# A two-layer attention trunk on one core: another order of blocks in paired weight groups, one weight sum on VectorE, side work behind the splits

## The chip, the core and the metric

One core of a Trainium2 chip runs the whole program. The metric is device time in microseconds (us); three runs were made, and one more execution was recorded by the hardware profiler. TensorE is the matrix engine, VectorE (DVE) and ScalarE (ACT) the elementwise engines, GpSimd is POOL, SyncE is SP; SBUF is the on-chip memory, PSUM holds TensorE's sums in eight banks.

## What is computed

A decoder trunk of two layers on 256 tokens of width 2048 in float32: one of gated linear attention (GLA, 4 heads), one of retention (8 heads). Cut to what matters here:

```python
def gla_mixer(h, w_in, w_a1, w_a2, b_a, head_g, w_out):
    q, k, v, gate = jnp.split(h @ w_in, [GLA_DK, 2 * GLA_DK, 2 * GLA_DK + D_INNER], axis=-1)
    ...                                   # decayed attention in chunks, norm of each head
    return (o * jax.nn.silu(gate)) @ w_out

def retention_mixer(h, positions, w_in, gn_g, gn_b, w_out):
    q, k, v, gate = jnp.split(h @ w_in, [RET_DK, 2 * RET_DK, 2 * RET_DK + D_INNER], axis=-1)
    q, k = apply_rotary(q, cos, sin), apply_rotary(k, cos, sin)
    ...                                   # scores with per-head decay, group norm of each head
    return (o * jax.nn.silu(gate)) @ w_out

for i in range(2):
    h = h + (gla_mixer, retention_mixer)[i](rms_norm(h, g[i]), ...)
return rms_norm(h, final_norm)
```

Nearly all of the work is the four large products with weights (`h @ w_in`, `o @ w_out` in each layer).

## The kernel before

**Weights.** All weights lie in HBM as groups of 2048 x 512. A group is four chunks of 512 rows (1 MB, tile `raw`, four buffers, loaded by SP's queue at L183). A chunk is two units of 256 rows, tiles 128x1024. A unit is split into two reduced-precision parts: `hi` by a copy on ScalarE (L216), `lo = raw - hi` on VectorE (L217); three buffers each. A product of exact factors is then three products (hi with hi, lo with hi, hi with lo: L277 to L279 in pairs). Units are numbered in the order in which they are used (`hi287`, `lo287`). `next_weights` writes the splits up to two units ahead of the products. A scheduler with a model of the engines sets the final order on each engine; each engine then works its queue in order.

**Groups and pairs.** Some groups are multiplied plainly (`group_w` for queries and keys, `rqk` in retention; `group_x`). Others come as pairs of groups gp and gq: for the upper half of the 2048 rows, the 2x2 block product of two token halves and two groups is made with seven products instead of eight. A list of blocks says the order: V0 to V3 and G0 to G3 are ordinary blocks of gp and gq over the lower half of the rows (each one unit, both token halves, 12 matmuls of 512 columns), S1 to S7 the seven products (each one chunk, so two units, one combination of tokens, also 12 matmuls). So an ordinary block needs one split, a seven-product block two.

The seven products need sums of weight chunks. They are made in place: after a chunk's unit is split, POOL issues a transfer of 0.5 MB from HBM that adds into the `raw` buffer (`accum_op`, L225). Buffer x holds gp's chunk 0 for S1, then with gq's chunk 0 added for S5, then with gq's chunk 1 for S6, then with gp's chunk 1 for S4. Buffer y holds gq's chunk 1 for S3, then with gq's chunk 0 for S7. S2 uses gp's chunk 1. With the two lower chunks of each group (V0/V1, V2/V3, G0/G1, G2/G3) a pair has seven chunks. There are 13 pairs: six in retention heads (value and gate groups, `rp`), seven in the output products (`ga`, `gb`: GLA's first and second half of inner columns; `ra`, `rb`: retention's), two per half but one in `rb`, whose other two groups are multiplied plainly.

**Sums in PSUM.** `pair_x` uses banks c11, c21, c12 (pool `acc`, four) and a, b (pool `lev`, two). S1's result in a is copied to c11 by ScalarE (L375), and V0 and S2 add there. Other partial results go to the caller's `on` function, which in the output half adds them to the residual (L916, L883) and in retention makes values and gates from them.

**Side work.** Rotary and scores (`ret_scores`), the head's norm (`o_part`), the transposes of its output (`og_part`, `transpose_out`) and the sums of tokens for pairs (`token_combos`) are generators in the queue `side`; `advance` runs one step after each unit or block. The scheduler is free to put such a step on ScalarE or VectorE ahead of splits. `o_part` of a paired head runs at once, at the first unit of the next head's `rqk`.

**Residual.** After each pair of the halves `gb` and `ra` half of the residual (1 MB) is stored to HBM (`held`, L931), because the buffer is used for the token sums `x1`, `x2` in between; it comes back at L1137.

Of the kernel before, what the change touches and what calls it, by code (L numbers as in the profile page):

```python
# [17 lines left out]
P = 128  # L18
# [37 lines left out]
def kernel(  # L56
# [63 lines left out]
    PAIR = ("S1", "V0", "S2", "V1", "S5", "S3", "V2", "G0", "S6", "G1", "S7", "V3", "S4", "G2", "G3")  # L120

    def plan_pair(gp, gq):
# [7 lines left out]
        for block in PAIR:  # L130
            kind, n = block[0], int(block[1])
            if kind in "VG":
                j, half = divmod(n, 2)
                c = chunk(kind + str(j), gp if kind == "V" else gq, 2 + j)
                units.append((c, half, half == 1, ()))
            elif n == 2:
                plan_units(plan_chunk(gp, 1))
            elif n in (3, 7):
                plan_units(chunk("y", gq, 1), n == 7, [(gq, 0)] if n == 3 else ())
            else:  # L140
                then = {1: [(gq, 0)], 5: [(gq, 1)], 6: [(gp, 1)], 4: ()}[n]
                plan_units(chunk("x", gp, 0), n == 4, then)

    def plan_all():
        g = 0
        for stage, heads in (("gla", 2), ("gla", 2), ("ret", 4), ("ret", 4)):
            for h in range(heads):
                plan_group(g)
                if stage == "ret" and h < heads - 1:
                    plan_pair(g + 1, g + 2)  # L150
                    g += 3
                    continue
# [4 lines left out]
            plan_pair(g, g + 1)  # L157
# [3 lines left out]
            else:  # L161
                plan_pair(g + 2, g + 3)
# [41 lines left out]
    def emit_split(pieces=1, between=None):  # L204
# [9 lines left out]
        for k in range(pieces):  # L214
            sl = slice(k * step, (k + 1) * step)
            a = nc.scalar.activation(hi[:, sl], src[:, sl], AF.Copy)  # L216
            b = nc.vector.tensor_tensor(lo[:, sl], src[:, sl], hi[:, sl].bitcast(F32), ALU.subtract)  # L217
            if i == 0:
# [11 lines left out]
    state = {"sub": 0}  # L230
    side = deque()

    def advance(n=1):
        for _ in range(n):
            while side:
                try:
                    next(side[0])
# [36 lines left out]

    def product(ps, a, hi, lo, q, start, stop):
        xh, xl = a
        mm(ps, xh, hi[:, q, :], start=start, stop=False, skip_group_check=True)  # L277
        mm(ps, xh, lo[:, q, :], start=False, stop=False, skip_group_check=True)  # L278
        mm(ps, xl, hi[:, q, :], start=False, stop=stop, skip_group_check=True)  # L279
# [46 lines left out]
    def pair_x(lhs, name, cname, on, late=None):  # L326

        a = lev_p.tile([P, GW], F32, tag="lev", name=f"{name}_psa")
        c11 = acc_p.tile([P, GW], F32, tag="acc", name=f"{name}_ps11")

        def seven(ps, get, start, stop):
            for half in range(2):
                hi, lo = next_weights()
                for q in range(SUB):
                    k = half * SUB + q
                    product(ps, get(k), hi, lo, q, start and k == 0, stop and k == CHUNK - 1)
# [5 lines left out]
        def mixed(n):  # L342
            return lambda k: tuple(x[:, k] for x in combos[cname][n])

        def both(ps, j, start, stop, second_first=False):
            hi, lo = next_weights()
            order = [(q, t) for q in range(SUB) for t in range(2)]
            if second_first:
                order = [(q, t) for t in (1, 0) for q in range(SUB)]
            for q, t in order:  # L350
                kt = 2 * CHUNK + j * SUB + q
                x = tuple(lhs[:, kt, i, t * P : (t + 1) * P] for i in range(2))
                product(ps[t], x, hi, lo, q, start[t] and q == 0, stop[t] and q == SUB - 1)
            advance()

        c21 = b = c12 = None
        for block in PAIR:
            kind, n = block[0], int(block[1])
            if kind == "V":
                if c21 is None:  # L360
                    c21 = acc_p.tile([P, GW], F32, tag="acc", name=f"{name}_ps21")
                if n == 2 and late is not None:
                    late()
                both((c11, c21), n, (False, n == 0), (n == 3, False), n == 0)
                if n == 3:
                    on("11", c11)
            elif kind == "G":
                both((c12, b), n, (False, False), (n == 3, n == 3))
                if n == 3:
                    on("12", c12)  # L370
                    on("22", b)
            elif n == 1:
                seven(a, plain(0, 0), True, True)
                with tc.high_priority():
                    nc.scalar.activation(c11, a, AF.Copy)  # L375
            elif n == 2:
                seven(c11, plain(1, 0), False, False)
            elif n == 5:
                while cname not in combos:
                    advance()  # L380
                b = lev_p.tile([P, GW], F32, tag="lev", name=f"{name}_psb")
                seven(b, mixed(0), True, True)
                on("q", b)
            elif n == 3:
                c12 = acc_p.tile([P, GW], F32, tag="acc", name=f"{name}_ps12")
                seven(c12, mixed(2), True, False)
            elif n == 6:
                seven(a, mixed(1), False, True)
                on("p2", a)
            elif n == 7:  # L390
                seven(a, mixed(3), False, True)
                on("p3", a)
# [37 lines left out]
    def evac_w(ps, dst, name):  # L430
        tmp = t4_p.tile([P, 4, SEQ], F32, tag="t4", name=f"{name}_h2")
        with tc.high_priority():
# [219 lines left out]
    def transpose_out(src, kt0, scale0, dst, name):  # L652
        for half in range(2):
# [7 lines left out]
            for jj in range(2):  # L661
                kt = kt0 + half * 2 + jj
                if scale0 is None:
                    nc.scalar.activation(dst[:, kt, 0, :], tp[:, jj, :], AF.Copy)
                    nc.vector.tensor_tensor(
                        dst[:, kt, 1, :], tp[:, jj, :], dst[:, kt, 0, :].bitcast(F32), ALU.subtract
                    )
                else:
# [222 lines left out]
    def out_half(first, final, name, later=None, keep_resid=False):  # L891
# [13 lines left out]
        for pair in range(1 if final else 2):  # L905
# [5 lines left out]
            def on(event, ps):  # L911
# [126 lines left out]
    def ret_scores(h, box):  # L1038
# [5 lines left out]
        nc.vector.tensor_tensor(a, qk, tb(0, 4), ALU.mult)  # L1044
        nc.vector.tensor_tensor(four(b)[:, :, 0, :], four(qk)[:, :, 1, :], tb(1, 2), ALU.mult)
        yield
        nc.vector.tensor_tensor(four(b)[:, :, 1, :], four(qk)[:, :, 0, :], tb(1, 2), ALU.mult)
        nc.vector.tensor_tensor(four(a)[:, :, 0, :], four(a)[:, :, 0, :], four(b)[:, :, 0, :], ALU.subtract)
# [9 lines left out]
        yield  # L1058
# [16 lines left out]
    def ret_head(h):  # L1075
# [6 lines left out]

        ps = group_w(xhl, f"rqk{h}", hook=late_o)
# [5 lines left out]
        evac_w(ps, qk, f"rqk{h}")  # L1089
# [10 lines left out]
        def o_part(v, o, bank):  # L1100
            drain_side()
            po = o_mms(hw["sc"], v, f"ro{h}", bank)
            if o is None:
                o = o_p.tile([P, 2, GW], F32, tag="o", name=f"ro{h}")
            bs = st_p.tile([P, 2, 6], F32, tag="bs", name=f"bs{h}")
            mv = st_p.tile([P, 2, 2], F32, tag="mv", name=f"mv{h}")
            for t in range(2):
# [4 lines left out]
                )  # L1112
# [190 lines left out]
```

## Time and profile before

| | before |
|---|---|
| runs, us | 1411.2, 1412.0, 1413.4 (median 1412.0) |
| profiled execution, us | 1413.7, span 1412.0 |
| granted TensorE clock, mean | 0.997 |
| TensorE / VectorE / ScalarE busy | 98% / 74% / 57% |
| transfers | 316.04 MB, mean 224 GB/s |

A group row of the profile reads: line, engine, operation, output <- inputs by the program's names, shape, count; then busy us, mean ns of one, idle us before. A row of waits: engine, line of the waiting instruction, what it waited for, us in total, times, longest. A row of transfers: names, queue, count, KB each, median us from issue to landing. A timeline row starts with start and duration in us and ends, in brackets, with the idle time before it and what ended it; a row of the chain of waits has start, duration, engine, name and line. A row of windows: the stretch, its length, busy us (and instructions) of TensorE, its weight loads, VectorE, ScalarE and GpSimd, the granted clock, the DMA engines' share, GB/s.

### The profile page before, as it was taken

The numbers are of one execution on the slowest core, as the hardware profiler recorded it, in microseconds if no ns is written. First come the engines' busy times: TensorE is split into PE (matmuls) and PEld (weight loads), VectorE is DVE, ScalarE is ACT, GpSimd is POOL, SyncE is SP. The second block draws the span as 40 slices with busy tenths as digits, with TensorE's granted clock in tenths as the row PEclk, the third lists the DMA queues.
The fourth block names the chain that finished last, engine by engine and source line by source line (L and its number), as shares of the span: only waits on it lengthen the run. The fifth ranks groups of instructions, "written<-read, shape, count | busy, mean of one in ns | idle before, by whom it ended". The sixth has DMA issues, their size and how long they took to land.

```text
span 1412.0 us, 17904 instructions
## 1 busy us (share of the span) xinstructions
PE 1380.2 (98%) x6644; PEld 1149.6 (81%) x6644; DVE 1037.8 (74%) x1477; ACT 800.6 (57%) x1019; POOL 190.6 (13%) x361
## 2 busy tenths in 40 slices
PE   8999999999999999999999999999899999999997
PEld 7888888778888888877888888887787878788877
DVE  6594887777845785788878787887667777778773
ACT  6665655654555656666655555455456565654563
POOL 1011030110000020211102020111101212110200
PEclk9999999999999999999999999999999999999999
DMA  9554555998555555799687969569988787874981
GB/s 349 207 183 145 197 173 179 205 285 271 175 171 184 184 186 180 197 301 283 207 269 204 264 201 325 199 195 271 240 297 219 254 219 256 228 305 164 225 295 62
DMA packets 54631, 316.04 MB, mean 224 GB/s; under 512 B 6400, under 2 KB 6912, under 8 KB 25232
## 3 DMA queue, kind: packets, MB, share of 16 engines
q1 hardware_dynamic: 34944, 243.42, 47.7%
q0 software_dynamic: 18592, 70.13, 24.3%
q10 hardware_dynamic: 1008, 1.35, 0.3%
q8 instruction: 52, 0.85, 0.2%
q14 instruction: 35, 0.29, 0.1%
HBM read 308.58 MB, written 6.29 MB: 223 GB/s over the span
## 4 chain that ended last, share of the span: by engine, by line
PE 74%; DMA 11%; DVE 7%; issue 4%; ACT 3%; POOL 1%; ACTq 0%; POOLq 0%; DVEq 0%
DMA raw<-in_w_all 11%; PE rqk_ps L421 8%; PE gv_ps L256 4%; PE gv_ps L257 4%; PE gv_ps L258 4%; DVE lo L217 4%; PE gg_ps L256 4%; PE rqk_ps L422 4%; PE gg_ps L258 4%; PE gg_ps L257 4%; PE gqk_ps L421 3%; ACT hi L216 2%; PE rp__ps L278 2%; PE rp__ps L279 2%; PE rp__ps L277 2%
## 5 line engine op out<-in xcount | busy, mean ns | idle before, releaser
L217 DVE TENSOR_TENSOR lo<-raw,hi 128x1024 fp32r<-128x1024 f32 (+1 forms) x551 | 667.0, 1223 | 294.0 <-ACT hi L216 288.8
L216 ACT ACTIVATE hi<-raw 128x1024 fp32r<-128x1024 f32 (+1 forms) x551 | 578.5, 1057 | 490.4 <-PE rqk_ps L421 86.5
L421 PE MATMUL rqk_ps<-xhl,hi 128*128 128x512 f32 x480 | 162.0, 396 | 0.0
L225 POOL DMA_DIRECT2D raw<-in_w_all x104 | 88.6, 852 | 390.4 <-DVE lo L217 370.9
L422 PE MATMUL rqk_ps<-xhl,lo 128*128 128x256 f32 x480 | 121.9, 282 | 0.0
L421 PEld LDWEIGHTS rqk_ps<-xhl,hi 128*128 128x128 f32 x480 | 87.7, 188 | 16.7
L257 PE MATMUL gv_ps<-lo,xhl 128*128 128x512 f32 x256 | 100.4, 392 | 0.0
L257 PE MATMUL gg_ps<-lo,xhl 128*128 128x512 f32 x256 | 100.4, 392 | 0.0
L258 PE MATMUL gv_ps<-hi,xhl 128*128 128x512 f32 x256 | 100.3, 392 | 0.0
L258 PE MATMUL gg_ps<-hi,xhl 128*128 128x512 f32 x256 | 100.0, 391 | 0.0
L256 PE MATMUL gv_ps<-hi,xhl 128*128 128x512 f32 x256 | 93.0, 391 | 0.0
L422 PEld LDWEIGHTS rqk_ps<-xhl,lo 128*128 128x128 f32 x480 | 87.9, 188 | 5.0
L256 PE MATMUL gg_ps<-hi,xhl 128*128 128x512 f32 x256 | 91.7, 391 | 0.0
L278 PE MATMUL rp__ps<-lo,xhl 128*128 128x512 f32 x192 | 75.8, 395 | 5.8 <-DVE lo L217 5.8
L279 PE MATMUL rp__ps<-hi,xhl 128*128 128x512 f32 x192 | 74.8, 390 | 0.0
L277 PE MATMUL rp__ps<-hi,xhl 128*128 128x512 f32 x192 | 71.7, 394 | 2.9 <-ACT rp__ps L375 2.9
L421 PE MATMUL gqk_ps<-xhl,hi 128*128 128x512 f32 x216 | 72.2, 396 | 0.0
L789 POOL TENSOR_TENSOR s<-s,m 128x64 f32<-128x64 f32 x56 | 32.3, 610 | 241.0 <-DVE m L780 187.9
L257 PEld LDWEIGHTS gv_ps<-lo,xhl 128*128 128x128 f32 x256 | 48.1, 188 | 9.7
L257 PEld LDWEIGHTS gg_ps<-lo,xhl 128*128 128x128 f32 x256 | 48.1, 188 | 9.6
L256 PEld LDWEIGHTS gv_ps<-hi,xhl 128*128 128x128 f32 x256 | 47.9, 188 | 9.9
L258 PEld LDWEIGHTS gg_ps<-hi,xhl 128*128 128x128 f32 x256 | 48.1, 188 | 9.6
(503 smaller groups left out, 2772.2 us busy)
## 6 DMA issues: line engine op xcount, KB each, us to landing
raw<-in_w_all SPq DMA_DIRECT2D x225, 1024.0 KB, 5.1
raw<-in_w_all POOLq DMA_DIRECT2D x104, 512.0 KB, 8.4
held<-resid POOLq DMA_DIRECT2D x4, 1024.0 KB, 8.2
resid<-held POOLq DMA_DIRECT2D x2, 2048.0 KB, 12.1
resid<-in_x_n SPq DMA_DIRECT2D x2, 1024.0 KB, 12.6
gg<-in_gn_g POOLq DMA_DIRECT2D x8, 256.0 KB, 4.1
gb<-in_gn_b POOLq DMA_DIRECT2D x8, 256.0 KB, 3.9
raw<-in_w_all SPq DMA_DIRECT2D x3, 512.0 KB, 6.7
```

The source lines that it names most:

```text
L216: a = nc.scalar.activation(hi[:, sl], src[:, sl], AF.Copy)
L217: b = nc.vector.tensor_tensor(lo[:, sl], src[:, sl], hi[:, sl].bitcast(F32), ALU.subtract)
L225: nc.gpsimd.dma_start(src, chunk_src(g, k)[:, rows], accum_op=ALU.add)
L256: mm(ps, xh, hi[:, q, :], start=kt == 0, stop=False)
L257: mm(ps, xh, lo[:, q, :], start=False, stop=False)
L258: mm(ps, xl, hi[:, q, :], start=False, stop=kt == NKT - 1)
L277: mm(ps, xh, hi[:, q, :], start=start, stop=False, skip_group_check=True)
L278: mm(ps, xh, lo[:, q, :], start=False, stop=False, skip_group_check=True)
L279: mm(ps, xl, hi[:, q, :], start=False, stop=stop, skip_group_check=True)
L421: mm(ps[c], wh, rhs[:, kt, :, :], start=kt == 0, stop=False)
L422: mm(ps[c][:, 0, :], wl, rhs[:, kt, 0, :], start=False, stop=False)
L789: nc.gpsimd.tensor_tensor(dst, dst, side_of(m[:, li, :]), ALU.add)
```

## The change

- Three block orders take the place of one. LATE (the first pair of an output half) and EARLY (the second) and SLOW (the retention heads) alternate ordinary and seven-product blocks.
- In LATE and EARLY the sum for S6 is x + y on VectorE, in two halves of 128x1024, when both S3 and S5 have been split; y then takes its own addition. In SLOW all additions stay with POOL.
- S1's result no longer goes to c11 by a copy: the caller takes it (`p1`), in the output half by an addition to the residual, in retention by an eviction to SBUF that is added when c11 is complete. Where G0 comes before S5 (LATE), the second output bank is one of its own and S5's result is added to the residual twice.
- From the first retention head on, side work and the eviction of `rqk` are held behind the latest split on ScalarE and VectorE; rotary, norm and output work are cut into more steps, and `o_part` goes to the side queue.
- `transpose_out` evicts two tiles at once where there is no scale. The residual is stored once per half, 2 MB.

```diff
-    PAIR = ("S1", "V0", "S2", "V1", "S5", "S3", "V2", "G0", "S6", "G1", "S7", "V3", "S4", "G2", "G3")
+    LATE = ("V0", "S1", "V1", "S2", "G0", "S5", "G1", "S3", "V2", "S6", "V3", "S7", "G2", "S4", "G3")
+    EARLY = ("V0", "S1", "V1", "S3", "V2", "S5", "V3", "S6", "G0", "S2", "G1", "S7", "G2", "S4", "G3")
+    SLOW = ("V0", "S1", "V1", "S3", "V2", "S5", "V3", "S2", "G0", "S6", "G1", "S7", "G2", "S4", "G3")
...
+        x, y = (gp, 0), (gq, 1)
+        both = None if order is SLOW else max(order.index("S3"), order.index("S5"))
...
+            elif pos == both:
+                then = [(at["x"], at["y"]), (at["y"], (gq, 0))]
+            elif both is None and n == 5:
+                then = [(at["x"], y)]
+            elif both is None and n == 3:
+                then = [(at["y"], (gq, 0))]
...
-        for g, k in then:
-            rows = slice(j * SUB, (j + 1) * SUB)
-            nc.gpsimd.dma_start(src, chunk_src(g, k)[:, rows], accum_op=ALU.add)
+            latest[:] = [a.ins, b.ins]
+        rows = slice(j * SUB, (j + 1) * SUB)
+        for to, what in then:
+            x = raws[to][:, rows]
+            if isinstance(what, int):
+                nc.vector.tensor_tensor(x, x, raws[what][:, rows], ALU.add)
+            else:
+                nc.gpsimd.dma_start(x, chunk_src(*what)[:, rows], accum_op=ALU.add)
...
+    def behind_splits():
+        with tc.issue_after(latest[0]), tc.issue_after(latest[1]):
+            yield
...
-                    next(side[0])
+                    with behind_splits() if state["behind"] else nullcontext():
+                        next(side[0])
...
-                with tc.high_priority():
-                    nc.scalar.activation(c11, a, AF.Copy)
+                on("p1", bank["a"])
...
+                shared = "22" not in bank
+                on("q", bank["b"], shared)
...
-            for jj in range(2):
-                kt = kt0 + half * 2 + jj
-                if scale0 is None:
-                    nc.scalar.activation(dst[:, kt, 0, :], tp[:, jj, :], AF.Copy)
...
+            if scale0 is None:
+                d = dst[:, kt0 + half * 2 : kt0 + half * 2 + 2]
+                nc.scalar.activation(d[:, :, 0, :], tp, AF.Copy)
+                nc.vector.tensor_tensor(d[:, :, 1, :], tp, d[:, :, 0, :].bitcast(F32), ALU.subtract)
...
+                if event == "p1":
+                    join(0, 0, ALU.add)
+                elif event == "q":
                     join(0, 1, ALU.subtract)
+                    if not shared:
+                        join(1, 1, ALU.add)
...
-            pair_x(ogt, f"{name}{pair}", name, on, drain_side)
-            if keep_resid:
-                cols = slice(2 * pair * GW, (2 * pair + 2) * GW)
-                nc.gpsimd.dma_start(held[:, :, cols], R["t"][:, :, cols])
+            pair_x(ogt, f"{name}{pair}", name, on, EARLY if pair else LATE, drain_side)
+        if keep_resid:
+            nc.gpsimd.dma_start(held, R["t"])
...
+        state["behind"] = True
         ps = group_w(xhl, f"rqk{h}", hook=late_o)
...
-        evac_w(ps, qk, f"rqk{h}")
+        with behind_splits() if paired else nullcontext():
+            evac_w(ps, qk, f"rqk{h}", not paired)
...
+            if event == "p1":
+                with tc.high_priority():
+                    nc.scalar.activation(o[:, 1, :], ps, AF.Copy)
+            elif event == "q":
...
             elif event == "11":
-                split_scaled(v[:, 0], ps, r2[:, 0:1])
+                with tc.high_priority():
+                    tt(o[:, 1, :], ps, o[:, 1, :], ALU.add)
+                split_scaled(v[:, 0], o[:, 1, :], r2[:, 0:1])
...
-        pair_x(xhl, f"rp{h}_", "x1" if h < 4 else "x2", on)
+        pair_x(xhl, f"rp{h}_", "x1" if h < 4 else "x2", on, SLOW)
...
-            o_part(v, o, (lev_p, "lev"))
+            side.append(o_part(v, o, (lev_p, "lev")))
```

What the change moves is seen in the order on the engines. First VectorE at the start of the second retention head's pair, before: `lo286` and `lo287` are S1's units, `lo288` is V0's; `rqk1` is the eviction of queries and keys, `rot0` the transposes of the head ahead, `ra1` and `rb1` the rotary.

```order
L217 TENSOR_TENSOR lo287_6391<-raw123_6283,hi287_6390 128x1024
L435 TENSOR_TENSOR rqk1_6411<-rqk1_ps0_6176,rqk1_h2_6412 128x256
L665 TENSOR_TENSOR ogt_107<-rot0_tp0_6245,ogt_107 128x256
L665 TENSOR_TENSOR ogt_107<-rot0_tp1_6274,ogt_107 128x256
L435 TENSOR_TENSOR rqk1_6411<-rqk1_ps1_6177,rqk1_h2_6412 128x256
L435 TENSOR_TENSOR rqk1_6411<-rqk1_ps2_6178,rqk1_h2_6412 128x256
L665 TENSOR_TENSOR ogt_107<-rot0_tp0_6245,ogt_107 128x256
L435 TENSOR_TENSOR rqk1_6411<-rqk1_ps3_6179,rqk1_h2_6412 128x256
L665 TENSOR_TENSOR ogt_107<-rot0_tp1_6274,ogt_107 128x256
L1044 TENSOR_TENSOR ra1_6454<-rqk1_6411,trig_108 128x1024
L1045 TENSOR_TENSOR rb1_6455<-rqk1_6411,trig_108 128x2x256
L1047 TENSOR_TENSOR rb1_6455<-rqk1_6411,trig_108 128x2x256
```

There `lo288` follows. After the change, at the same place (`lo287` and `lo288` are S1's units, V0's `lo286` stands ahead):

```order
L233 TENSOR_TENSOR lo287_6392<-raw124_6311,hi287_6391 128x1024
L473 TENSOR_TENSOR rqk1_6412<-rqk1_ps0_6180,rqk1_h2_6413 128x256
L702 TENSOR_TENSOR ogt_107<-rot0_tp0_6333,ogt_107 128x2x256
L702 TENSOR_TENSOR ogt_107<-rot0_tp1_6360,ogt_107 128x2x256
L473 TENSOR_TENSOR rqk1_6412<-rqk1_ps1_6181,rqk1_h2_6413 128x256
L473 TENSOR_TENSOR rqk1_6412<-rqk1_ps2_6182,rqk1_h2_6413 128x256
L473 TENSOR_TENSOR rqk1_6412<-rqk1_ps3_6183,rqk1_h2_6413 128x256
L233 TENSOR_TENSOR lo288_6432<-raw124_6311,hi288_6431 128x1024
L1084 TENSOR_TENSOR ra1_6448<-rqk1_6412,trig_108 128x1024
L233 TENSOR_TENSOR lo289_6453<-raw123_6265,hi289_6452 128x1024
```

The rotary has moved behind the split, one step between two splits; the eviction and the transposes have stayed ahead of it.

Second, SP's loads in the same pair. In brackets stand the semaphores that a load waits for; the one of a DMA (DMAHW) names the buffer, since it is that on which the buffer's earlier chunk landed. Before, `raw126` is y, `raw127` the chunk of V2 and V3, `raw128` that of G0 and G1:

```order
L183 DMA raw124_6325<-in_w_all 128x2048 [waits DMAHW1_49,DVE_49]
L183 DMA raw125_6367<-in_w_all 128x2048 [waits DMAHW2_49,DVE_49]
L183 DMA raw126_6430<-in_w_all 128x2048 [waits DMAHW3_49,DVE_49]
L183 DMA raw127_6442<-in_w_all 128x2048 [waits DMAHW6_49,DVE_49]
L183 DMA raw128_6535<-in_w_all 128x2048 [waits DMAHW5_49,DVE_49]
```

After, `raw124` is x, `raw125` is y, `raw126` the chunk of V2 and V3, `raw127` S2's, `raw128` that of G0 and G1:

```order
L199 DMA raw124_6311<-in_w_all 128x2048 [waits DMAHW1_49,DVE_49]
L199 DMA raw125_6367<-in_w_all 128x2048 [waits DMAHW2_49,DVE_49]
L199 DMA raw126_6389<-in_w_all 128x2048 [waits DMAHW3_49,DVE_49]
L199 DMA raw127_6462<-in_w_all 128x2048 [waits DMAHW4_49,DVE_49]
L199 DMA raw128_6496<-in_w_all 128x2048 [waits DMAHW7_49,DVE_49]
```

Before, HW5 is the landing of `raw124`, the chunk of V0 and V1, used up at `lo291`; after, HW7 is that of `raw126`, used up at `lo295`, while `raw128` is first split as `hi297` before and `hi298` after.

Third, VectorE in the second pair of the first half (EARLY) after the change: `lo109` and `lo110` are S5's units, `lo111` is V3's (from `raw50`), `lo115` is S2's first (from `raw52`, whose load waits for `lo111`).

```order
L233 TENSOR_TENSOR lo110_2706<-raw48_2504,hi110_2705 128x1024
L244 TENSOR_TENSOR raw48_2504<-raw48_2504,raw49_2554 128x1024 x2
L233 TENSOR_TENSOR lo111_2725<-raw50_2567,hi111_2724 128x1024
L233 TENSOR_TENSOR lo112_2735<-raw48_2504,hi112_2734 128x1024
L953 TENSOR_TENSOR resid0_104<-resid0_104,ga1_psb_2723 128x512
L233 TENSOR_TENSOR lo113_2747<-raw48_2504,hi113_2746 128x1024
L233 TENSOR_TENSOR lo114_2766<-raw51_2623,hi114_2765 128x1024
```

Before, at units 108 to 111 (S5 and S3), the order had only splits:

```order
L217 TENSOR_TENSOR lo108_2649<-raw47_2402,hi108_2648 128x1024
L217 TENSOR_TENSOR lo109_2665<-raw47_2402,hi109_2664 128x1024
L217 TENSOR_TENSOR lo110_2689<-raw50_2587,hi110_2688 128x1024
L217 TENSOR_TENSOR lo111_2700<-raw50_2587,hi111_2699 128x1024
L916 TENSOR_TENSOR resid0_104<-resid0_104,ga1_psb_2685 128x512
```

The two sums now stand between S5's second split and V3's.

More of the change, by code (lines that the diff above doesn't have):

```diff
@@ L128, in chunk @@
             return at[key]
-        for block in PAIR:
+        x, y = (gp, 0), (gq, 1)
+        both = None if order is SLOW else max(order.index("S3"), order.index("S5"))
+        for pos, block in enumerate(order):
             kind, n = block[0], int(block[1])
@@ L135, in plan_pair @@
                 units.append((c, half, half == 1, ()))
-            elif n == 2:
+                continue
+            if n == 2:
                 plan_units(plan_chunk(gp, 1))
[L138 to L142, printed above, removed]
+                continue
+            c = chunk("y", *y) if n in (3, 7) else chunk("x", *x)
+            then = []
+            if n == 1:
+                then = [(at["x"], (gq, 0))]
+            elif n == 6:
+                then = [(at["x"], (gp, 1))]
+            elif pos == both:
[4 more added lines that the diff above has]
+                then = [(at["y"], (gq, 0))]
+            plan_units(c, n in (4, 7), then)
     def plan_all():
@@ L324, with pair_x, take, wrote @@
     combos = {}
[L326 to L331, printed above, removed]
+    def pair_x(lhs, name, cname, on, order, late=None):
+        bank = {}
+        left = {"11": 5, "21": 5, "12": 5, "22": 4}
+        def take(key, pool, tag):
+            if key not in bank:
+                bank[key] = pool.tile([P, GW], F32, tag=tag, name=f"{name}_ps{key}")
+                return True
+            return False
+        def wrote(key):
+            left[key] -= 1
+            if left[key] == 0:
+                on(key, bank[key])
+        def product(ps, a, hi, lo, q, start, stop):
+            xh, xl = a
+            mm(ps, xh, hi[:, q, :], start=start, stop=False, skip_group_check=True)
+            mm(ps, xh, lo[:, q, :], start=False, stop=False, skip_group_check=True)
+            mm(ps, xl, hi[:, q, :], start=False, stop=stop, skip_group_check=True)
+        def seven(key, get, start, stop):
             for half in range(2):
@@ L335, in seven @@
                     k = half * SUB + q
-                    product(ps, get(k), hi, lo, q, start and k == 0, stop and k == CHUNK - 1)
+                    product(bank[key], get(k), hi, lo, q, start and k == 0, stop and k == CHUNK - 1)
             advance()
@@ L342, in mixed, with both @@
         def mixed(n):
+            while cname not in combos:
+                advance()
             return lambda k: tuple(x[:, k] for x in combos[cname][n])
-        def both(ps, j, start, stop, second_first=False):
+        def both(keys, j):
+            start = [take(key, acc_p, "acc") for key in keys]
+            stop = [left[key] == 1 for key in keys]
             hi, lo = next_weights()
[L347 to L353, printed above, removed]
+            for q in range(SUB):
+                for t in range(2):
+                    kt = 2 * CHUNK + j * SUB + q
+                    x = tuple(lhs[:, kt, i, t * P : (t + 1) * P] for i in range(2))
+                    product(bank[keys[t]], x, hi, lo, q, start[t] and q == 0, stop[t] and q == SUB - 1)
+            for key in keys:
+                wrote(key)
@@ L354, in both @@
             advance()
-        c21 = b = c12 = None
-        for block in PAIR:
+        for block in order:
             kind, n = block[0], int(block[1])
[L359 to L362, printed above, removed]
+            if kind in "VG":
+                if block == "V2" and late is not None:
                     late()
[L364 to L371, printed above, removed]
+                both(("11", "21") if kind == "V" else ("12", "22"), n)
@@ L372, in pair_x @@
             elif n == 1:
[L373 to L375 removed]
+                take("a", lev_p, "lev")
+                seven("a", plain(0, 0), True, True)
+                on("p1", bank["a"])
             elif n == 2:
[L377 removed]
+                seven("11", plain(1, 0), False, left["11"] == 1)
+                wrote("11")
             elif n == 5:
[L379 to L380 removed]
```

77 lines of the change are left out of this document (42 added, 35 removed).

## The prediction

> **What bounds the kernel now.** I read the page's first part, then the waits of TensorE, then those places in the timeline.
>
> ```profile
> PE 1380.2 (98%) x6644; PEld 1149.6 (81%) x6644; DVE 1037.8 (74%) x1477; ACT 800.6 (57%) x1019; POOL 190.6 (13%) x361
> q0 software_dynamic: 18592, 70.13, 24.3%
> raw<-in_w_all SPq DMA_DIRECT2D x225, 1024.0 KB, 5.1
> raw<-in_w_all POOLq DMA_DIRECT2D x104, 512.0 KB, 8.4
> held<-resid POOLq DMA_DIRECT2D x4, 1024.0 KB, 8.2
> resid<-held POOLq DMA_DIRECT2D x2, 2048.0 KB, 12.1
> ```
>
> TensorE is busy for 1380.2 of 1412.0 us. The matmuls stay, so the change can only win waits. This is the whole list of TensorE's waits inside pairs:
>
> ```profile
> PE rp__ps L278 <- DVE lo L217: 5.8, 9, 1.0
> PE ra_ps L277 <- ACT hi L216: 4.0, 2, 3.1
> PE rp__ps L277 <- ACT rp__ps L375: 2.9, 6, 0.5
> PE ga_ps L277 <- ACT hi L216: 2.1, 2, 1.4
> PE gb_ps L278 <- DVE lo L217: 1.5, 4, 0.8
> PE ra_ps L278 <- DVE lo L217: 0.8, 1, 0.8
> PE ga_ps L278 <- DVE lo L217: 0.8, 1, 0.8
> PE rb_ps L278 <- DVE lo L217: 0.8, 1, 0.8
> PE gb_ps L277 <- ACT gb_ps L375: 0.5, 1, 0.5
> PE rb_ps L277 <- ACT hi L216: 0.4, 1, 0.4
> PE rot_tp L658 <- DVE ro L1128: 0.2, 1, 0.2
> ```
>
> They sum to 19.8 us in 29 waits. Each costs more than it shows, since matmuls overlap:
>
> ```profile
> 268.10 0.39 PE L278 MATMUL ga_ps<-lo,c_d 128*128 128x512 f32 x1
> 268.32 0.39 PE L279 MATMUL ga_ps<-hi,c_d 128*128 128x512 f32 x1
> 269.34 0.50 PE L277 MATMUL ga_ps<-hi,c_d 128*128 128x512 f32 x1 [0.63 <-ACT hi L216]
> 270.94 0.40 PE L279 MATMUL ga_ps<-hi,c_d 128*128 128x512 f32 x1
> 271.18 0.40 PE L277 MATMUL ga_ps<-hi,c_d 128*128 128x512 f32 x1
> ```
>
> Starts normally lie 0.227 us apart, 1.02 here: 0.79 lost where 0.63 is shown, and the matmul after it starts 0.11 late. So 0.27 us more per wait, 29 x 0.27 = 7.8. The 3.1 us wait has a follower:
>
> ```profile
> 1012.00:1016.00 4.00, 4.00 (x12) 3.13 (x11) 1.53 (x2) 0.24 (x2) 0.84 (x1) 0.57 1.01 181
> ```
>
> After the matmul counts the granted clock is the third number from the end: 0.57 over 4 us, 1.7 us of work lost. In all 19.8 + 7.8 + 1.7 = 29.3 us can be won, 12.7 of it in the six pairs of the retention heads (8.7 + 15 x 0.27), 16.6 in the seven of the output halves.
>
> **The retention pairs' start.** VectorE, then the matmul that waits:
>
> ```profile
> 756.65 1.23 DVE L217 TENSOR_TENSOR lo<-raw,hi 128x1024 fp32r<-128x1024 f32 x1 [1.81 <-ACT hi L216]
> 758.79 0.75 DVE L435 TENSOR_TENSOR rqk<-rqk_ps,rqk_h 128x256 f32<-128x256 f32 x2
> 760.45 1.22 DVE L1044 TENSOR_TENSOR ra<-rqk,trig 128x1024 f32<-128x1024 f32 x1
> 761.58 0.69 DVE L1045 TENSOR_TENSOR rb<-rqk,trig 128x512 f32<-128x512 f32 x1
> 762.78 2.36 DVE L217 TENSOR_TENSOR lo<-raw,hi 128x1024 fp32r<-128x1024 f32 x2
> 764.06 0.50 PE L278 MATMUL rp__ps<-lo,xhl 128*128 128x512 f32 x1 [0.98 <-DVE lo L217]
> ```
>
> Between lo287 and lo288 stand eight 128x256 operations (757.8 to 760.45, 0.33 each) and three of the rotary (1.13, then two of 0.60 up to 762.78): 5.0 us. After the change there remain four of 0.33 and two merged ones, each at the 0.60 of a 128x512: 2.5. The split comes 2.5 us earlier. It is also needed 1.4 us later, since TensorE first has half of S1 and the whole of V0 (18 products of 0.227) where it had S1's 12. The wait here, 0.98 + 0.51 + 2 x 0.27 = 2.0, goes with 1.9 to spare, and the copy at L375 with it. Its successor (six evictions to SBUF on ScalarE, six additions of 0.60 on VectorE) has four blocks, 11 us, before the output products need it: nothing on the path.
>
> **What is late next.** A load that comes after the split which frees its buffer can hold the array up. It has happened once, in the second pair of the first half (start, duration; the load takes 9.20):
>
> ```profile
> 303.15 1.24 DVE lo L217
> 304.40 9.20 DMA raw<-in_w_all
> 313.70 1.06 ACT hi L216
> 314.81 0.50 PE ga_ps L277
> ```
>
> A pair's seven chunks share four buffers. In a SLOW pair G0's chunk (raw128) now takes the buffer of V2/V3, free only after V3's split, lo295. Take V2's start on TensorE as 0. hi295 needs the buffer of hi292, which 13 products leave at 2.95 + 0.16 = 3.1; ScalarE's 1.06 and VectorE's 1.23 end it at 5.4. The load takes L. Then hi298 is there at 5.4 + 0.1 + L + 1.06 = 6.6 + L, lo298 at 7.8 + L. TensorE arrives after V2, S5, V3, S2 (4 x 12 x 0.227 = 10.9) and some 1.2 of score products (six of half the width and two small ones, an estimate from the 0.227), at 12.1, and needs the lo part three products later, at 12.8. The wait is L - 5.0. Before, that chunk took V0/V1's buffer, with three blocks between V1 and G0 where now one lies between V3 and G0, 5.4 us more, and no wait of the list stands there. SP issues in order, so the loads behind raw128 wait with it; they need buffers that come free later still.
>
> L is not the page's median of 5.1, which is over all stages. Medians of 1 MB loads among accumulating transfers, 768 to 798 us and 315 to 337 us:
>
> ```profile
> raw<-in_w_all SPq DMA_DIRECT2D x5, 1024.0 KB, 7.5
> raw<-in_w_all SPq DMA_DIRECT2D x5, 1024.0 KB, 7.3
> ```
>
> S5's two accumulations go out just ahead of raw128, but S3's and S1's have mostly landed: a little better than those, I take 7.2. Bounds are 5.1 and 9.2. SLOW: 2.2 us, times six 13.2.
>
> EARLY has it twice. S2's chunk waits for V3's split, which now stands behind the two weight sums (2 x 1.13). From V2's start the split ends at 5.9; with 1.2 for ScalarE and 1.2 for VectorE behind the load, lo115 is there at 8.3 + L, needed after five blocks and a product at 13.8: L - 5.5 = 1.7. G2's chunk follows S2's: 0.9 by the same working. 2.6 x 3 = 7.8.
>
> LATE releases every buffer six blocks or more ahead. What stays is in the first pair: ScalarE's decay work ahead of a split,
>
> ```profile
> 266.94 1.28 ACT L691 ACT_TABLE_LOAD   x1
> 268.23 1.06 ACT L216 ACTIVATE hi<-raw 128x1024 fp32r<-128x1024 f32 x1
> ```
>
> and this is not moved (the flag for side work is set only at the first retention head). I take 1.1 there, for 1.4 + 2 x 0.27 = 1.9 before, and 0.3 in each of the other three: 2.0.
>
> **The other parts.** Weight sum: 14 accumulating transfers go, 14 sums of 1.22 us come, 2.4 us of VectorE in pairs of 41. One transfer holds all engines for about 24.3% x 1412 / 104 = 3.3 us (an upper bound, the queue has a few others), so a pair gets 6.6 us back. It has work for that:
>
> ```profile
> 297.00:337.00 40.00, 38.56 (x171) 31.50 (x170) 29.22 (x28) 23.14 (x23) 5.42 (x7) 1.00 1.01 268
> 759.00:804.00 45.00, 43.24 (x192) 34.72 (x191) 35.57 (x42) 27.66 (x33) 5.66 (x8) 1.00 0.90 250
> ```
>
> The second number from the end is the DMA engines' share, 1.01 in that output pair, 0.90 in a retention pair; VectorE, the third busy time, has 29.2 of 40 and 35.6 of 45 us, so the sums are covered but not far from their limit. That is why L stays high: three quarters of the accumulations remain, in SLOW all. Residual additions (p1 in seven pairs, one more in LATE, 0.6 each) run beside products. 16 merged evictions save some 0.1 us each on VectorE and ScalarE: nothing on the path.
>
> Residual store: two of 2 MB for four of 1 MB, out of the crowded second pair, where the first pair's store stood in POOL's queue ahead of accumulations. ScalarE waits for it:
>
> ```profile
> 1046.32 2.01 ACT L305 ACTIVATE x_d<-x_c 128x1024 fp32r<-128x1024 f32 x2 [2.57 <-DMA held<-resid]
> ```
>
> Bound by 8.2 and by the 12.1 of the opposite 2 MB transfer, it lands up to 3.9 us later; the combination now stands two units (5.5 us) later on ScalarE. I take nothing; bounds 0 and 2 x 3.9.
>
> **The sum.** Before 29.3; after 13.2 + 7.8 + 2.0 = 23.0; won 6.3. The profiled execution took 1413.7 (span 1412.0), the runs' median is 1412.0, 1.7 below it: about 1406 on the median's scale. Break-even lies where 2.0 + 6(L - 5.0) + 3(L - 4.6) reaches 29.3 (EARLY's S2 term and its 0.9 together are L - 4.6): L = 7.9.
>
> **Rivals.** (1) Loads land as in quiet stages, L = 5.1. For it: fewer transfers in the output halves, S1, S3 and S5 no longer bunched. Then SLOW costs 0.6 in all, EARLY about 1.5, LATE 2: 25 won, 1387. Against: the 7.3 and 7.5.
> (2) Slower: raw128 meets S5's accumulations as 304.40 did, L = 9.2. SLOW then costs 6 x 4.2 = 25.2, EARLY 3 x 4.6 = 13.8, with LATE 41.0: 1424. Waits of 4.2 exceed the 3.1 after which the clock fell; with 1.7 each in the six pairs, 1434. It decides from L = 7.9 on. [...]
> (3) No change to measure: the retention pairs give back at G0 what they win at the start, and EARLY the rest; L between 7.6 and 8.2, 1412. Here 0.2%, 2.8 us, is what a measurement of this kernel can tell from none.
> That VectorE's queue is not cleared is out: the order shows it.
>
> **How the numbers follow.** Forecast (L 6.2 to 7.6, 1397 to 1409): 0.48. Rival 1 and its neighbourhood, below 1397: 0.18. Rival 3: 0.15. Rival 2: 0.19. Faster 0.48 + 0.18 = 0.66, same 0.15, slower 0.19. The range goes from rival 1's 1388 to 1420, into rival 2.
>
> **What would show it.** Right: no wait at V0 of retention pairs, none on ScalarE's copy; a wait of hi or lo in G0 of SLOW, in S2 and G2 of EARLY, each behind a weight load of over 6 us; 90 accumulating transfers; LATE nearly without waits. Wrong: those loads land in 5 us, or the waits of G0 pass 3 us and the granted clock drops; or S6 waits for accumulations that VectorE's sums made late.

## The result, and the profile after

| | before | changed |
|---|---|---|
| median of the runs, us | 1412.7 (1411.2 to 1413.7) | 1445.0 (1442.7 to 1449.1) |
| ratio to before, 95% interval | | 1.0233 (1.0202 to 1.0263) |
| profiled execution, span, us | 1412.0 | 1445.6 |
| granted TensorE clock, mean | 0.997 | 0.982 |
| accumulating transfers | 104 | 90 |

The change costs 2.3%, where 1406 and a gain were forecast. The page of the changed kernel, TensorE's busy time and the transfers:

```profile
PE 1395.2 (97%) x6644; PEld 1160.9 (80%) x6644; DVE 1064.3 (74%) x1492; ACT 796.6 (55%) x996; POOL 179.8 (12%) x345
raw<-in_w_all POOLq DMA_DIRECT2D x90, 512.0 KB, 7.6
held<-resid POOLq DMA_DIRECT2D x2, 2048.0 KB, 12.1
```

The same 6644 matmuls are busy 15.0 us longer: part of them ran at a lower clock (the mean is 0.982 where it was 0.997). TensorE's waits inside pairs, in total, times and longest:

```profile
PE rp__ps L366 <- ACT hi L232: 23.8, 6, 4.6
PE ra_ps L366 <- ACT hi L232: 4.3, 1, 4.3
PE ga_ps L366 <- ACT hi L232: 4.2, 1, 4.2
...
PE ga_ps L367 <- DVE lo L233: 1.6, 3, 0.6
PE gb_ps L367 <- DVE lo L233: 1.4, 2, 0.8
PE ra_ps L367 <- DVE lo L233: 0.8, 2, 0.5
PE rb_psa L367 <- DVE lo L233: 0.6, 1, 0.6
PE ra_psa L367 <- DVE lo L233: 0.6, 1, 0.6
PE gb_ps L366 <- ACT hi L232: 0.4, 2, 0.2
...
```

Before there were 29 small waits, none over 3.1 us. Now 8 waits of about 4 us hold nearly everything: one in each of the six retention pairs, one in the second pair of `ga` and of `ra`. The chain of waits shows one of the six (start, duration):

```profile
711.94 1.24 DVE lo L233
...
713.19 9.11 DMA raw<-in_w_all
...
722.41 1.06 ACT hi L232
...
723.52 0.55 PE rp__ps L366
```

V3's split ends, the load of G0's chunk starts in the buffer that this frees and lands 9.11 us later; then `hi`, then the product. The windows of that load and of the 4 us behind it (granted clock third from the end, the DMA engines' share, GB/s):

```profile
713.20:722.30 9.10, 6.70 (x33) 5.29 (x31) 3.22 (x4) 1.68 (x3) 0.57 (x1) 1.00 1.05 293
723.40:727.40 4.00, 3.88 (x9) 2.73 (x10) 3.90 (x5) 2.98 (x5) 0.65 (x1) 0.57 0.20 80
```

The DMA engines are full (1.05) during the load that the array comes to wait for, and mostly idle afterwards (0.20), while the array works at clock 0.57.

To follow the time by stage I add up, from the timeline, how far the starts of successive matmuls lie apart beyond their 0.227 us (0.117 at 256 columns). This loss, in us, per half and for the six retention pairs together, in one profiled execution each (numbers of the experiments as below):

| | ga | gb | six rp | ra | rb | sum | ratio to before |
|---|---|---|---|---|---|---|---|
| before | 3.8 | 3.9 | 14.0 | 8.1 | 1.9 | 31.7 | 1 |
| changed | 10.2 | 4.2 | 40.1 | 10.1 | 1.8 | 66.4 | 1.0233 (1.0202 to 1.0263) |
| 1 spread, retention | 8.5 | 4.8 | 12.7 | 9.1 | 2.4 | 37.5 | 1.0057 (1.0036 to 1.0078) |
| 2 spread, also halves | 9.5 | 5.9 | 13.4 | 4.5 | 2.0 | 35.3 | 1.0002 (0.9978 to 1.0026) |
| 3 no S5 addition | 10.6 | 5.1 | 4.1 | 11.5 | 2.8 | 34.1 | 1.0019 (0.9998 to 1.0041) |
| 4 nothing held behind splits | 10.4 | 12.6 | 38.1 | 9.6 | 1.7 | 72.4 | 1.0285 (1.0251 to 1.0318) |
| 5 spread, all sums on VectorE | 5.7 | 1.9 | 10.4 | 10.5 | 4.0 | 32.5 | 0.9960 (0.9944 to 0.9976) |
| 6 spread, sums in halves | 5.4 | 0.8 | 8.7 | 5.5 | 3.1 | 23.5 | 0.9963 (0.9947 to 0.9979) |
| 7 old order in retention | 9.9 | 4.2 | 0.7 | 8.7 | 1.9 | 25.4 | 1.0012 (0.9994 to 1.0030) |
| 8 as 5, LATE in all halves | 3.4 | 1.9 | 10.5 | 8.0 | 2.3 | 26.1 | 0.9974 (0.9960 to 0.9988) |
| 9 old in retention, spread second pairs | 2.5 | 2.3 | 0.7 | 3.4 | 2.3 | 11.2 | 0.9882 (0.9864 to 0.9900) |
| 10 old order everywhere | 3.5 | 0.4 | 3.2 | 5.5 | 6.3 | 18.9 | 0.9915 (0.9895 to 0.9935) |
| 11 as 7, nothing held | 11.6 | 9.6 | 13.1 | 9.0 | 0.5 | 43.8 | 1.0076 (1.0053 to 1.0098) |

66.4 less 31.7 is 34.7, against 33.6 between the two spans. Single executions of one kernel lie up to 1% apart (before: 1404.7 to 1418.1), so kernels are compared by the recorded ratio of their runs to before's on the same chip, which lies within 0.2% of the quotient of the medians. A loss in the table, from one execution, need not match the median.

### The profile page after: what moved, and what is told of

It reads as the page before. It is cut to its first block, busy times and chain, and to the rows that moved or that the text cites. A ratio compares the mean times of both kernels' runs of the same rounds, so it can differ in the third digit from the quotient of the medians.

```text
span 1445.6 us, 17834 instructions
## 1 busy us (share of the span) xinstructions
PE 1395.2 (97%) x6644; PEld 1160.9 (80%) x6644; DVE 1064.3 (74%) x1492; ACT 796.6 (55%) x996; POOL 179.8 (12%) x345
## 4 chain that ended last, share of the span: by engine, by line
PE 82%; DMA 9%; DVE 4%; ACT 2%; issue 1%; POOL 1%; ACTq 0%; POOLq 0%; DVEq 0%
DMA raw<-in_w_all 9%; PE rqk_ps L459 7%; PE gg_ps L284 4%; PE gv_ps L284 4%; PE gv_ps L286 4%; PE gv_ps L285 4%; PE gg_ps L285 4%; PE gg_ps L286 4%; PE rqk_ps L460 4%; PE gqk_ps L459 3%; PE rp__ps L366 3%; PE rp__ps L368 3%; PE rp__ps L367 3%; DVE lo L233 3%; ACT hi L232 2%; PE gqk_ps L460 2%
## 5 line engine op out<-in xcount | busy, mean ns | idle before, releaser
L246 POOL DMA_DIRECT2D raw<-in_w_all x90 | 78.0, 867 | 372.7 <-DVE lo L233 323.3
L366 PE MATMUL rp__ps<-hi,xhl 128*128 128x512 f32 x192 | 75.3, 407 | 23.8 <-ACT hi L232 23.8
L368 PE MATMUL rp__ps<-hi,xhl 128*128 128x512 f32 x192 | 77.1, 402 | 0.0
L366 PEld LDWEIGHTS rp__ps<-hi,xhl 128*128 128x128 f32 x192 | 37.3, 194 | 33.8 <-ACT hi L232 26.4
## 6 DMA issues: line engine op xcount, KB each, us to landing
resid<-held POOLq DMA_DIRECT2D x2, 2048.0 KB, 10.4
resid<-in_x_n SPq DMA_DIRECT2D x2, 1024.0 KB, 10.9
```

Source lines behind the costliest of these rows:

```text
L246: nc.gpsimd.dma_start(x, chunk_src(*what)[:, rows], accum_op=ALU.add)
```

## The experiments

**Theory A.** A load waits for the split that frees its buffer, then lands late because accumulating transfers stand ahead of it, and the wait lowers the clock. **Rival B.** Work held behind the splits delays splits. **Rival C.** A retention pair has too many transfers, in whatever order.

**1. The blocks spread in the retention pairs.** Every buffer is released four blocks or more before it is needed:

```diff
-    SLOW = ("V0", "S1", "V1", "S3", "V2", "S5", "V3", "S2", "G0", "S6", "G1", "S7", "G2", "S4", "G3")
+    SLOW = ("V0", "S1", "V1", "S2", "V2", "S5", "V3", "S3", "G0", "S6", "G1", "S7", "G2", "S4", "G3")
```

> The order of the retention pairs becomes V0 S1 V1 S2 V2 S5 V3 S3 G0 S6 G1 S7 G2 S4 G3, so that every weight buffer is released four blocks or more before the chunk that takes it is needed; nothing else changes. Theory A (the load of G0's chunk starts only when V3 is split and then lands some 9.7 us later): the six waits of about 4 us at G0 and the clock drops behind them go, the loss in the retention pairs falls from 40.1 us to under 8, about 1412 us. Rival B (the side work behind the splits holds up splits on VectorE or ScalarE): the loss stays about where it is, 1440 or more. Rival C (the transfer queue itself is too slow for a retention pair, wherever a load stands): a wait of some us comes back at S6, S7 or G2, 1425 to 1435.

Measured 1420.6 us, where theory A said about 1412 and rival C 1425 to 1435; before was 1410.9 on this chip. The retention pairs' waits (three lines of TensorE's list):

```profile
PE rp__ps L367 <- DVE lo L233: 3.5, 5, 0.8
PE rp__ps L366 <- ACT hi L232: 3.0, 6, 1.0
...
PE rp__psa L367 <- DVE lo L233: 1.0, 2, 0.8
```

The 4 us waits are gone, and with them 27 of 40.1 us. Rival B is out. Not all went as A expected: 12.7 us stay where under 8 was said, in waits of up to 1 us, as rival C has them but smaller.

**2. The same in the second pairs.** The edit gives EARLY the same row of blocks. With that the two orders became one and the same tuple, so that the test for SLOW also held in the second pairs: their VectorE sum went back to transfers (96), which the expectation did not foresee.

> The same order also in the second pair of each output half (with VectorE's sum after S3). Theory A: also the two waits of 4.2 to 4.4 us in the second pairs of the first and the third half go, with about 1 us behind each and 2 us of clock, about 15 us less than the run before in this call: 1397 us, below the 1412.7 of the kernel before. Rival B: 1430 or more. Rival C: the waits move to S7 or S4, 1405 to 1425.

Measured 1413.0 us, level with before, where A said 1397. The waits of about 4 us in `ga` and `ra` are gone; most of those that stay in the second pairs and in retention are for S4, which needs x's last addition. So rival C, with waits at S4 and 1405 to 1425, was the nearer one here. The addition issued at 725.0 us, in the first retention pair (one transfer, its landing time last):

```profile
raw<-in_w_all POOLq DMA_DIRECT2D x1, 512.0 KB, 11.5
```

**3. Fewer transfers at the same place.** The order SLOW stays; S5's addition is left out of the retention pairs, so S6 and S4 there multiply an incomplete sum:

```diff
-            elif both is None and n == 5:
+            elif both is None and n == 55:
```

> The changed kernel without the addition of gq's chunk 1 into x after S5 in the retention pairs (12 of the 90 accumulating transfers left out; S6 and S4 of these pairs multiply a wrong sum). The load of G0's chunk starts at the same place behind V3's split. Theory A with the backlog of transfers as the cause of the long landing: it lands in 5 to 7 us in place of 9.7, the wait at G0 is 0 to 2.2 us (landing time less 5.0), no clock drop: 1410 to 1420 us. If the landing time does not come from the accumulations: 9 us and more, waits of 4 us stay, 1440. Rival B: waits stay as well, 1440.

Measured 1415.3 us. In the first retention pair, the loads of G0's and G2's chunks (median landing last); then TensorE's only wait in the first three pairs:

```profile
raw<-in_w_all SPq DMA_DIRECT2D x2, 1024.0 KB, 4.9
```

```profile
PE rp__psa L366 <- ACT hi L232: 0.2, 1, 0.2
```

G0's chunk lands in 5.0 us in place of 9.1, and nothing waits for it. The load stands at the same place, behind V3's split. So the late buffer alone does no harm here; it needs the two additions just ahead of the load. The loss of the six pairs is 4.1 us.

**4. Nothing held behind splits.**

```diff
-                    with behind_splits() if state["behind"] else nullcontext():
+                    with nullcontext():
...
-        with behind_splits() if paired else nullcontext():
-            evac_w(ps, qk, f"rqk{h}", not paired)
+        with nullcontext():
+            evac_w(ps, qk, f"rqk{h}")
```

> The changed kernel with side work and the eviction of rqk placed as before, not held behind the latest split. Theory A: the waits at G0 of the retention pairs stay at about 4 us with the clock drops, and a wait of about 1 us on VectorE's split at V1 or S1 may come back at the start of these pairs: 1443 to 1455 us. Rival B (work held behind splits made the changed kernel slow): the waits at G0 shrink below 2 us, 1415 to 1425.

Measured 1453.4 us. The retention pairs lose 38.1, as in the changed kernel; rival B falls a second time. The start of these pairs does not wait either, since V0 stands ahead of S1. A 6.1 us wait is new in `gb`. Without the holding, token sums for `x1` (L309) come between the splits of the second pair there, and V3's split comes behind both of VectorE's weight sums, where in the changed kernel it stood between them. Both of y's additions are then out before the load, at 643.8 and 645.3 against 645.9, and it lands in 11.0 us (7.5 in the changed kernel, with one addition ahead). Run 11, with the same edit, has the same order there and 9.2.

**5 to 8.** Run 5 makes the sum on VectorE in all pairs, run 6 in the output halves alone, both with the spread order; run 7 gives the retention pairs their old order; run 8 is run 5 with LATE in the second pairs too.

```diff
  # run 5; run 6 keeps the old line, with two tuples of the spread order
-        both = None if order is SLOW else max(order.index("S3"), order.index("S5"))
+        both = max(order.index("S3"), order.index("S5"))
  # run 7
+    SLOW = ("S1", "V0", "S2", "V1", "S5", "S3", "V2", "G0", "S6", "G1", "S7", "V3", "S4", "G2", "G3")
  # run 8, beside the edits of run 5
-            pair_x(ogt, f"{name}{pair}", name, on, EARLY if pair else LATE, drain_side)
+            pair_x(ogt, f"{name}{pair}", name, on, LATE, drain_side)
```

> The spread order of blocks in the retention pairs and in the second pairs, with the sum x + y made by VectorE after S3 in all 13 pairs: 78 accumulating transfers. (In the second run of this study, with 96 transfers, the second pairs had lost VectorE's sum as well, so that S4 waited 0.5 to 1.1 us for x's last addition, landing 11.5 us after its issue.) Theory A (waits come from loads and additions landing late behind each other): with two transfers fewer per pair they land in 5 to 7 us, the waits at S4 go, the loss in the retention pairs is 4 to 6 us in all and in the second pairs under 1.5 each: 1396 to 1402 us, faster than before by about 0.8%. Rival (VectorE's two sums of 1.1 us each hold up the splits in retention pairs, where VectorE is the busiest): a wait of 1 us on lo at G0 or S6 in each retention pair, 1408 to 1415.

> The spread order in the retention pairs with all additions by transfer, and in the second pairs with VectorE's sum: 90 transfers. It differs from the run before in this call by the sum in retention alone, from the second run of this study by the sum in the second pairs alone. Theory A: the retention pairs lose 9 to 13 us as in the first two runs, the second pairs under 1.5 each: 1403 to 1408. Rival (the sum on VectorE gains nothing): 1411 to 1416, as the second run.

> The changed kernel with the block order of before in the retention pairs (S1 V0 S2 V1 S5 S3 V2 G0 S6 G1 S7 V3 S4 G2 G3); first and second pairs of the output halves, the side work behind the splits and the caller's taking of S1 stay as changed. Theory A: no wait at G0, the loss in the retention pairs is what the side work behind the splits and the missing copy leave of the 14.0 us of before: 3 to 8 us, so 1408 to 1414, with the waits of the second pairs as in the changed kernel. If the start of the retention pairs gains nothing from the side work: 14 us, 1419. If the order was not to blame: 1440.

> As the first run of this call, but with the order of the first pairs (LATE) in the second pairs too. LATE releases every weight buffer six blocks or more ahead, but issues y's two and x's two additions within 6 us behind S3 with a load behind them. Theory A: the same as the first run within 4 us, 1396 to 1404, with a wait of about 1 us twice in S4. Rival (a second output bank of its own in the second pair, which keeps a bank from the next product): some us more at the start of the product behind it, 1405 to 1412.

Measured 1405.7, 1404.9, 1411.6 and 1407.5 us, before 1410.3. Runs 6 and 7 lie where they were expected; run 5 missed its 1396 to 1402, and run 8 lies in the range of its rival. Run 6 beside run 2: VectorE's sum in the second pairs is worth about 0.4%, from 1.0002 to 0.9963. The size is rough: the two intervals touch, and the retention pairs, the same in both, differ by 4.7 us between the two profiled executions. Run 5 beside run 6: in the retention pairs it is worth nothing. Its waits there, and those of run 6:

```profile
PE rp__ps L367 <- DVE lo L233: 6.6, 11, 0.8
```

```profile
PE rp__ps L367 <- DVE lo L233: 3.5, 5, 0.8
...
PE rp__ps L366 <- ACT hi L232: 1.2, 3, 0.5
```

Two fewer transfers per pair take away waits for data and put others for VectorE in their place. Run 8 beside run 5 shows no gain of LATE over the spread order (0.9974 and 0.9960). Run 7 was the surprise: with the old order and the work held behind splits, the retention pairs lose 0.7 us in all. One of them in a window:

```profile
695.00:737.00 42.00, 42.00 (x190) 34.49 (x189) 35.63 (x41) 28.03 (x34) 6.59 (x8) 1.00 0.96 265
```

TensorE is busy 42.00 of 42.00 us, with eight accumulating transfers in the pair.

**9 to 11.** Run 9 joins the best parts: old order in retention, LATE in the first pairs, spread in the second. Run 10 has the old order in all three tuples and `both = None`, so 104 transfers. Run 11 is run 7 with the edit of run 4.

```diff
  # run 9
-    EARLY = ("V0", "S1", "V1", "S3", "V2", "S5", "V3", "S6", "G0", "S2", "G1", "S7", "G2", "S4", "G3")
-    SLOW = ("V0", "S1", "V1", "S3", "V2", "S5", "V3", "S2", "G0", "S6", "G1", "S7", "G2", "S4", "G3")
+    EARLY = ("V0", "S1", "V1", "S2", "V2", "S5", "V3", "S3", "G0", "S6", "G1", "S7", "G2", "S4", "G3")
+    SLOW = ("S1", "V0", "S2", "V1", "S5", "S3", "V2", "G0", "S6", "G1", "S7", "V3", "S4", "G2", "G3")
```

> The block order of before in the retention pairs (which lost 0.7 us in all in the seventh run), LATE in the first pairs, the spread order with VectorE's sum in the second pairs (whose halves lost 5.4, 0.8, 5.5 and 3.1 us in the sixth run). Theory A (the changed kernel's loss is the buffer released too late in SLOW and EARLY, and nothing else in the change costs): the losses of the pairs add up to about 15 us, against 55 in the first profile of the changed kernel and 31.7 before, so 17 us less than before: 1393 to 1398, faster by 0.9 to 1.2%. Rival (something else in the change costs time outside the pairs, or waits come back in the halves with other transfers beside them): 1401 or more.

> The changed kernel with the block order of before in all 13 pairs and all additions by transfer (104): what stays of the change is the side work behind the splits, the caller's taking of S1, the merged evictions and the residual stored once. Theory A: the retention pairs lose under 2 us in all, the halves as before, 17.7 us or somewhat less without the copy: 12 us less than before, 1396 to 1401. Rival (what was won in the retention pairs came from fewer transfers elsewhere): 1407 or more.

> The seventh run (block order of before in the retention pairs) without the holding of side work and of the eviction of rqk behind the splits; S1's result still goes to the caller without the copy. If the holding removed the waits at the start of the retention pairs: their loss goes from 0.7 us back towards the 14.0 of before, 10 to 13 us, so 1420 to 1425. If it was the copy: loss stays under 5 us, 1411 to 1416.

Measured 1396.0, 1400.5 and 1423.4 us, each within its expected range; before 1413.3. Run 9 is 1.2% faster than before and 3.4% faster than the changed kernel (0.9882 / 1.0233, the two ratios from two chips). Its whole list of waits in pairs:

```profile
PE ra_ps L367 <- DVE lo L233: 1.3, 2, 0.7
PE ga_ps L367 <- DVE lo L233: 1.3, 2, 0.8
PE gb_ps L367 <- DVE lo L233: 1.3, 2, 0.8
PE ra_psa L367 <- DVE lo L233: 0.6, 1, 0.6
PE rb_psa L367 <- DVE lo L233: 0.6, 1, 0.6
PE rb_ps L366 <- ACT hi L232: 0.4, 1, 0.4
PE ga_ps L366 <- ACT hi L232: 0.2, 1, 0.2
```

Run 11 brings the waits at the start of the retention pairs back, 13.1 us of loss against 0.7. VectorE there without the holding, and with it:

```profile
1073.44 1.23 DVE L1084 TENSOR_TENSOR ra<-rqk,trig 128x1024 f32<-128x1024 f32 x1
1074.58 0.68 DVE L1086 TENSOR_TENSOR rb<-rqk,trig 128x512 f32<-128x512 f32 x1
1075.18 0.69 DVE L1088 TENSOR_TENSOR rb<-rqk,trig 128x512 f32<-128x512 f32 x1
1075.78 2.35 DVE L233 TENSOR_TENSOR lo<-raw,hi 128x1024 fp32r<-128x1024 f32 x2
```

```profile
1061.40 2.36 DVE L233 TENSOR_TENSOR lo<-raw,hi 128x1024 fp32r<-128x1024 f32 x2 [0.52 <-ACT hi L232]
1063.68 1.22 DVE L1084 TENSOR_TENSOR ra<-rqk,trig 128x1024 f32<-128x1024 f32 x1
1064.81 1.22 DVE L233 TENSOR_TENSOR lo<-raw,hi 128x1024 fp32r<-128x1024 f32 x1
```

## Why the prediction was wrong

**The place and the formula were right.** "The wait is L - 5.0" for G0 of a SLOW pair: the six loads landed in 9.11, 10.14, 9.48, 9.12, 9.75 and 9.21 us, and the gaps between matmuls were 3.78, 4.80, 4.15, 3.79, 4.42 and 3.88 beyond the 0.227, each 0.3 below L - 5.0. "L - 5.5" for S2 of EARLY: the loads of `ga`, `gb` and `ra`

```profile
raw<-in_w_all SPq DMA_DIRECT2D x1, 1024.0 KB, 10.8
```

```profile
raw<-in_w_all SPq DMA_DIRECT2D x1, 1024.0 KB, 7.5
```

```profile
raw<-in_w_all SPq DMA_DIRECT2D x1, 1024.0 KB, 10.9
```

give 5.3, 2.0 and 5.4; measured were 4.4 + 1.0, 0.4 + 1.0 and 4.4 + 1.0 (the wait for `hi` and the one for `lo`). The 0.9 forecast for G2's chunk was not seen in `ga` and `ra`.

**The term that failed is L = 7.2.** It was taken from medians of loads "among accumulating transfers", and set a little lower because S3's and S1's additions had mostly landed. That much was so: of these only S3's second was under way, for another 1.8 us. But S5's two had gone out 4.1 and 1.8 us ahead of the load, and took 8.6 and 11.3 us to land. In 697 to 745 us of the changed kernel POOL's queue and SP's took these shares of the engines (packets, MB, share):

```profile
q0 software_dynamic: 1216, 4.39, 50.0%
q1 hardware_dynamic: 935, 6.87, 38.7%
raw<-in_w_all SPq DMA_DIRECT2D x7, 1024.0 KB, 7.7
raw<-in_w_all POOLq DMA_DIRECT2D x8, 512.0 KB, 8.1
```

50.0% of 48 us for 4.39 MB is 2.9 us of all engines for an addition (512 KB, 0.52 MB), 38.7% for 6.87 MB is 2.8 us for a load (1024 KB, 1.05 MB). The prediction had the first of these (at most 3.3) and used it only for VectorE's sum. Two additions and the load add up to 8.6 us, well over 7.2. That sum is no rule for the landing time and lay below it each time: one addition and the load make 5.7, the load alone 2.8, where 7.5 (`gb`) and 5.0 (run 3) were measured.

How the 9.11 us come about stands in the trace. The load is issued at 713.19; from 713.2 to 716.2 only POOL's queue (q0) moves packets, from 717 to 720 both queues do (two windows; a packet counts in the window in which it starts, so a share can pass 100%):

```profile
q0 software_dynamic: 179, 0.64, 107.7%
```

```profile
q0 software_dynamic: 78, 0.32, 52.5%
q1 hardware_dynamic: 77, 0.63, 51.9%
```

In run 3 the load is issued at 714.99, and SP's queue has 68.3% of the engines from 714.5 to 719. So in the SLOW pair the load first got nothing for over 3 us, and then half. In `gb`, where one addition stood ahead, POOL's queue has 92.8% of the first 2.6 us (644.4 to 647) and SP's 91.1% of the next 2.5. Landing times by the additions unlanded at issue bear it out: 5.0 with S5's left out (run 3), 7.5 with one (`gb`), 9.1 to 10.9 with two (S5's in SLOW, y's in `ga` and `ra`). From 717 to 720 the two queues had about equal shares (52.5% and 51.9%), in the load's first three microseconds POOL's had all (107.7%); why the load got nothing in them no run here shows.

**The clock.** The forecast had no wait over 3 us, hence no drop. Rival 2 had it at 1.7 us a pair. The six gaps add up to 24.8 us; the other 15.3 of the 40.1 us, 2.5 a pair, lie almost all in the slow products behind them (granted clock 0.50 to 0.57 over the 4 us behind each). Rival 2 with its 25.2 for SLOW was right on the waits. Its whole loss, 41.0 + 10.2 = 51.2, is 15.2 short of the 66.4: 5.1 by the clock (15.3 for 10.2) and 10.5 in the output halves (26.3 for 15.8). Its L = 9.2 was in part luck, since the load at 304.40 that it came from had met something else: a plain load issued at 302.14 stood ahead of it, and the next additions went out behind it, at 306.03 and 307.39.

**Point by point.** SLOW: 13.2 forecast, 40.1 measured. EARLY and LATE together: 9.8 forecast, 26.3 measured, with two clock drops (0.50 over the 4 us from 324.7 in `ga` and from 1038.3 in `ra`). LATE alone kept one gap of 0.7 to 0.8 us in each half, 3.0 for the 2.0 forecast. The start of the retention pairs: 12.7 were to be won, and no wait is left there; in SLOW V0's place ahead of S1 does it (run 4), in the old order the holding (0.7 in run 7 against 13.1 in run 11). Leaving out the copy at L375 won little by itself: run 11 has no copy either and loses 13.1 where 14.0 were lost before. The residual stored once cost nothing that can be seen on TensorE; ScalarE's wait for it fell from 2.57 us to

```profile
ACT x_d L327 <- DMA held<-resid: 1.3, 2, 0.8
```

VectorE's sum, "covered but not far from their limit": so it was in the retention pairs (run 5), while it paid in the second pairs (run 6). No wait of S6 appeared; in `ga` V3's split, behind the two sums, held TensorE for 0.6 us.

## What to carry to other kernels

A landing time is not a property of a transfer: a load of 1 MB landed here in 5.0, 7.5 and 9.1 to 10.9 us, by what was unlanded when it was issued. Add up the engine time of that and of the load, take the sum as a lower estimate (here 2.8, 5.7 and 8.6), and do this at the one place where it is needed, not from a stage's median. An order of work that releases a buffer only one block before its next use, and behind a burst of transfers, can cost more than the many small waits that it removes: 40.1 us in the six retention pairs here, 14.0 before. Here the new orders did the damage: with the orders and sums of before (run 10) the rest of the change was worth 0.9%, and 1.2% with LATE in the first pairs and the spread order in the second, both with VectorE's sum (run 9).

## What the hardware showed beyond that

An accumulating transfer of 0.5 MB occupied the engines as long (2.9 us) as a plain load of 1 MB (2.8 us).

The clock also fell after much shorter waits than before (3.1 us). Run 2, in `ga` (two timeline rows, and the window behind them):

```profile
291.44 0.51 PE L366 MATMUL ga_ps<-hi,ogt 128*128 128x512 f32 x1 [0.76 <-ACT hi L232]
292.70 0.50 PE L367 MATMUL ga_ps<-lo,ogt 128*128 128x512 f32 x1 [0.75 <-DVE lo L233]
```

```profile
292.70:296.70 4.00, 4.00 (x11) 3.17 (x12) 3.60 (x4) 1.65 (x2) 0.00 (x0) 0.57 0.76 260
```

Two waits of 0.76 and 0.75 us, one product between them, and 0.57 for 4 us. In run 10 two waits of 3.25 us each were followed by different clocks (the two rows, then the two windows):

```profile
943.03 0.50 PE L367 MATMUL ra_ps<-lo,ogt 128*128 128x512 f32 x1 [3.25 <-DVE lo L233]
1304.23 0.80 PE L367 MATMUL rb_ps<-lo,ogt 128*128 128x512 f32 x1 [3.25 <-DVE lo L233]
```

```profile
943.00:947.00 4.00, 3.96 (x17) 3.26 (x18) 4.00 (x6) 1.07 (x2) 0.00 (x0) 1.00 0.68 164
1304.00:1308.00 4.00, 3.77 (x9) 3.01 (x10) 4.00 (x6) 0.00 (x0) 0.00 (x0) 0.50 0.73 175
```

So the same wait of 3.25 us was followed by a clock of 1.00 once and of 0.50 another time, and 1.5 us of waiting within 2.4 us by 0.57 in run 2. How much waiting lowers the clock no run here shows.
